# Five edits at the seams between the phases of one encoder step

## The chip, the cores and the metric

One core of one Trainium2 chip runs the whole step as one program. Its five engines take their instructions in order, each from its own list: TensorE (PE in the profile, with its weight loads as PEld), VectorE (DVE), ScalarE (ACT), GpSimd (POOL) and SyncE (SP), which here does nothing but issue DMAs. The metric is device time in microseconds (us), the median of several runs.

## The reference, cut to what matters

One layer of a streaming encoder for 1024 prompt tokens and 8 samples of 16 tokens (1152 tokens, 9 blocks of 128, or 3 blocks t of 384):

```python
xn = rms_norm(x, norm_g)
u, g_pool, c_q, c_kv, k_r, g_mla = jnp.split(xn @ w_in, SPLIT_IDX, axis=-1)
pool_out = multiscale_pool(pool_hist, u, pos0, w_pool, pool_scale) * jax.nn.silu(g_pool)
q = (rms_norm(c_q, q_norm_g) @ w_uq).reshape(B, T, N_HEADS, D_NOPE + D_ROPE)
q_nope = rms_norm(q[..., :D_NOPE], q_nope_g)
q_rope = apply_rope(rms_norm(q[..., D_NOPE:], q_rope_g), cos[:, None], sin[:, None])
ckv_new = rms_norm(c_kv, kv_norm_g)
krope_new = apply_rope(rms_norm(k_r, k_rope_g), cos, sin)
ckv_all = jnp.concatenate([ckv_hist, ckv_new], axis=1)
kv = (ckv_all @ w_ukv).reshape(B, S, N_HEADS, D_NOPE + D_V)
k_nope = rms_norm(kv[..., :D_NOPE], k_nope_g)
attn = chunk_causal_attention(q_nope, q_rope, k_nope, krope_all, v, q_pos, jnp.arange(S))
mla_out = attn.reshape(B, T, D_MLA) * jax.nn.silu(g_mla)
h = x + jnp.concatenate([pool_out, mla_out], axis=-1) @ w_out
gate = jax.nn.sigmoid(rms_norm(h, ple_norm_g) @ w_ple_gate + b_ple_gate)
y = h + gate * (p @ w_ple)
```

`multiscale_pool` takes, for 4 groups of 256 channels, the mean over the last 2, 4, 8 or 16 tokens minus the token, and a 256x256 matrix for each group (the mixer). For the samples, 1024 past tokens come from a cache. All values are float32.

## The kernel before

**Precision.** Each fp32 operand is split into two halves in TensorE's reduced fp32 format: ScalarE casts the high half (L68, or L71 with a gain) and VectorE subtracts it from the source for the low half (L69, L72). Each product is then three matmuls (`mm3`, L77 to L79; in the input projection L175 to L177). [...]

**Input projection (`phase1`).** Weights stand as 128x128 blocks, tokens stream in blocks of 384. The 16 blocks of the inner dimension are taken in two chunks of 8, `chunk(0, ...)` and then `chunk(1, ...)`. In a chunk, two column tiles of the weight and two token blocks make a 2x2 block product, done with seven products instead of eight (`Quick.pair`), on sums and differences of the operands; the third token block is multiplied plainly by `X` (8 tiles, `last_block`). Chunk 0's results go to DRAM (`part1`) and come back as `q` in chunk 1 (`prior`), where ScalarE adds them into PSUM ahead of the product (L192). The operands of chunk 1 (seven kinds `OPS`, four tiles each) are made during chunk 0, stored to DRAM as `sums`, and loaded between the chunks through four tiles `a0` to `a3`, each kind's tile j through `aj` (L506); `put` splits them. `X` of chunk 1 follows, loaded through the three tiles `o`, which also hold the evictions.

**The end of a product (`finish`).** VectorE adds the part of chunk 0, or multiplies by the norm factor `R2` for the third token block (L531); `gp` and `gm` get a SiLU on ScalarE (L537) and are stored from ScalarE's queue, `u`, `cq` and `ckv` from GpSimd's (L539).

**Mixer (`Pool`).** In chunk 1, `mixer(m, i)` is called at up to four places i of each pair m. From m = 5 on, each second pair adds the steps of one mixer group g to a list, at i = 0, and each call takes two steps from it. The steps load `u` from DRAM (L708 and on), compute the windows on VectorE (`d`), split `d` into `dh` and `dl`, load the gates `gp` into `ev` (L720), multiply on TensorE into `aux` (12 matmuls for each token block), and store `mixp` from GpSimd's queue. The last products of the third token block are held back (`held`) so that they stand behind the mixer and run to the end of the phase.

**Keys and queries (`phase2`).** For each block j of 128 tokens: `keys(j)` makes keys and values in banks `pb` (5 banks) and stores `vv`; `keys_out` transposes keys over `pt` (2 banks) and stores `kT`; `queries(j)`, `queries_out`, `rotary_out` do the like for queries and store `qT` and `qrT`. All these stores go out on SP's queue. The weights `w_uq` come in eight loads through two tiles `raw` and are split into `wqh`, `wql`. The embedding product `p @ w_ple` (`Embed.block`, banks `p`, evictions L803, loads on ScalarE's queue) is put between the blocks as filler.

**Attention.** `attend_samples` starts with the cache of the samples: `cache_T` is loaded on SP, cast to `ch` and `cl`, and multiplied into `k`. At its end four groups g of two heads are multiplied by the value weights: the outputs of g = 0, 1 lie in bank 0 of `ob` and those of g = 2, 3 in bank 1; VectorE multiplies each by its gate (L1455). `attend_prompt` and `phase5` (output projection, gate) follow.

**What sets the order.** The program is traced as written, and a scheduler then simulates it and gives each engine one list, by when it thinks that each instruction can start. `tc.issue_after(ins)` says that what is traced in its block, on the engine of `ins`, is issued behind `ins`. DMAs are issued in the order of the list of the engine whose queue they are on, and a DMA whose data is not there yet holds up all behind it on that engine.

Of the kernel before, what the change touches and what calls it, by code (L numbers as in the profile page):

```python
# [1 line left out]

# [4 lines left out]
F32R = mybir.dt.float32r  # L7
# [12 lines left out]
P = 128  # L20
# [232 lines left out]
def phase1(k, sc):  # L253
# [35 lines left out]
    def o_tile():  # L289
        return k.t(xp, [P, TB], "o", bufs=3)  # L290
# [10 lines left out]
    def last_block(c, j):  # L301

        i = 8 * c + j
        raw = (o_tile() if c else k.t(rp, [P, 2 * TB], f"x{j}"))[:, :TB]
        nc.sync.dma_start(raw, io["xT"][2][:, i, :])
        hl = [k.t(xp, [P, TB], f"X{j}{x}", F32R) for x in "hl"]
        k.split(hl[0][:], hl[1][:], raw, k.norm_g[:, i:i + 1])
        if c == 0:
            squares(R2, raw, raw)
        return hl  # L310
# [189 lines left out]
    chunk(0, None, keep, prepare)  # L500


    qk.tail()
    for n in OPS:
        for j in range(4):
            raw = k.t(ap, [P, TB], f"a{j}")  # L506
            nc.sync.dma_start(raw[:], sc["sums"][:, 4 * OPS.index(n) + j, :])
            put(n, j, raw[:])
    hs.close()
    X = [last_block(1, j) for j in range(8)]  # L510

    def prior(i, t):
        q = k.t(ep, [P, TB], "q", bufs=3)
# [10 lines left out]
    def finish(i, t, ps, q):  # L524
        kind, n = kinds[i] if i < KR else ("kr", 0)
        o = o_tile()
        if q is not None:
            nc.vector.tensor_tensor(o[:], ps, q[:], ALU.add)
            ps = o[:]
        if t == 2:  # L530
            nc.vector.tensor_tensor(o[:], ps, R2[:], ALU.mult)  # L531
        if kind == "kr":
            k.later(rope_key(k, lp, aux_bank, o, kc, ks, t, sc))
            return
        store = nc.gpsimd
        if kind in ("gp", "gm"):
            nc.scalar.activation(o[:], o[:], AF.Silu)  # L537
            store = nc.scalar
        store.dma_start(sc[kind][t][:, n, :], o[:])  # L539
        if kind not in ("ckv", "cq"):  # L540
            return
        if (kind, t) not in acc:
            acc[kind, t] = [k.t(lp, [P, TB], f"acc{t}"), 2 if kind == "ckv" else 4]
            nc.scalar.activation(acc[kind, t][0][:], o[:], AF.Square)
        else:
            sq = k.t(lp, [P, TB], "sq")
            nc.scalar.activation(sq[:], o[:], AF.Square)
            nc.vector.tensor_tensor(acc[kind, t][0][:], acc[kind, t][0][:], sq[:], ALU.add)
        acc[kind, t][1] -= 1
        if not acc[kind, t][1]:  # L550
            k.later(latent_factor(kind, t, acc[kind, t][0]))
# [1 line left out]
    lp = ls.enter_context(tc.tile_pool(name="p1c", bufs=1, side="right", reuse_waits="tile"))  # L553
    kc = k.t(lp, [P, 9, DR], "kc")
    ks = k.t(lp, [P, 9, DR], "ks")
    rope_tables(k, lp, kc, ks, io["k_rope_g2"], 1.0)
    mix = []


    def mixer(m, i):  # L560
        k.tick()
        if m < 5:
            return
        if not mix:
            assert not k.queue
            ls.close()
            mp = es.enter_context(tc.tile_pool(name="p1p", bufs=1, side="right", reuse_waits="tile"))
            inv = k.t(mp, [P, 16], "inv")
            nc.sync.dma_start(inv[:], io["inv_cnt"])
            mix.append(Pool(k, mp, aux_bank, inv, sc, wp))  # L570
            mix[0].zero = k.t(mp, [P, 16], "zero")
            nc.vector.memset(mix[0].zero[:], 0.0)
        pool = mix[0]
        if m in (5, 7, 9, 11) and i == 0:
            g = (m - 5) // 2
            for t in range(NT):
                if t == 0:
                    pool.fetch(2 * g, 0)
                steps.append(lambda t=t: (pool.fetch(2 * g + 1, t), t and pool.gates(g, t - 1), pool.tile(2 * g, t)))
                steps.append(lambda t=t: pool.tile(2 * g + 1, t))  # L580
                if t:
                    steps.append(lambda t=t: pool.mix(g, t - 1))
                else:
                    steps.append(lambda: pool.weights(g))
                steps.append(lambda t=t: (t < NT - 1 and pool.fetch(2 * g, t + 1), pool.split()))
                if t == NT - 1:
                    steps.append(lambda: (pool.gates(g, NT - 1), pool.mix(g, NT - 1)))
        step(2)
# [240 lines left out]
def phase2(k, sc, sh, fill):  # L829
# [70 lines left out]
    def keys(j):  # L900

        ch, cl, _ = ckv[j]
        kn = k.t(pw, [P, H, DN], "kn")
        vv = k.t(pw, [P, H, DN], "vv")
        for c in range(4):
            ps = bank("pb")
            w = (wk, wv)[c // 2]
            sl = slice((c % 2) * 512, (c % 2 + 1) * 512)
            for rt in range(2):
                k.mm3(ps[:], ch[:, rt, :], cl[:, rt, :], w[0][:, rt, sl], w[1][:, rt, sl], rt == 0, rt == 1)  # L910
            hs = slice(4 * (c % 2), 4 * (c % 2) + 4)
            src = ps[:].rearrange("p (h d) -> p h d", h=4)
            if c < 2:
                nc.scalar.activation(kn[:, hs, :], src, AF.Copy)
            else:
                nc.scalar.activation(vv[:, hs, :], src, AF.Copy)
        nc.sync.dma_start(sc["v"][:, :, j, :].rearrange("h p d -> p h d"), vv[:])
        r, = inv_norms(kn[:])
        halves(kn[:], r)
        return j, kn  # L920

    def keys_out(j, kn):
        kT = k.t(pw, [P, H, P], "T", bufs=2)
        for c in range(2):
            a = bank("pt")
            for i in range(4):
                nc.tensor.transpose(a[:, i * P:(i + 1) * P], kn[:, 4 * c + i, :], k.ident[:])
            nc.scalar.activation(kT[:, 4 * c:4 * c + 4, :], a[:].rearrange("p (h d) -> p h d", h=4), AF.Copy)
        nc.sync.dma_start(sc["kT"][:, :, j * P:(j + 1) * P].rearrange("h p q -> p h q"), kT[:])

    def queries(j):

# [16 lines left out]
    def queries_out(j, qn):  # L949
# [6 lines left out]
                nc.tensor.transpose(a[:, i * P:(i + 1) * P], qn[:, 4 * c + i, :DN], k.ident[:])  # L956
            nc.scalar.activation(qT[:, 4 * c:4 * c + 4, :], a[:].rearrange("p (h d) -> p h d", h=4), AF.Copy, scale=gqk[:])
        if j < 8:
            nc.sync.dma_start(sc["qT"][:, :, pos].rearrange("h p q -> p h q"), qT[:])
        return qT  # L960

    def rotary_out(j, qr):
# [79 lines left out]
    pp = es.enter_context(tc.tile_pool(name="p2p", bufs=1, space=PSUM, reuse_waits="tile"))  # L1042
    pq = es.enter_context(tc.tile_pool(name="p2c", bufs=1, reuse_waits="tile"))
    pw = es.enter_context(tc.tile_pool(name="p2b", bufs=1, reuse_waits="tile"))
    cq = {8: latent("cq", 8, 4, k.q_norm_g)}
    wq = [(k.t(pq, [P, 4, TB], f"wqh{g}", F32R), k.t(pq, [P, 4, TB], f"wql{g}", F32R)) for g in range(4)]
    for g in range(4):
        for i in range(2):
            sl = slice(2 * i, 2 * i + 2)
            k.split(wq[g][0][:, sl, :], wq[g][1][:, sl, :], raw_w([P, 2, TB], io["w_uq"][g][:, sl, :])[:])  # L1050
    ckv[8] = latent("ckv", 8, 2, k.kv_norm_g, "8", 1)
    qc = k.t(pq, [P, 9, DR], "qc")
    qs = k.t(pq, [P, 9, DR], "qs")
    rope_tables(k, pq, qc, qs, io["q_rope_g2"], SCALE)

    def key_steps(j):
        kp = keys(j)
# [231 lines left out]
def attend_samples(k, sc, sh, between, fill):  # L1289
# [149 lines left out]
    for g in range(4):  # L1439
# [2 lines left out]
        wvh = k.t(bp, [P, 2, 2 * DN], "wvh", F32R, bufs=3)  # L1442
        wvl = k.t(bp, [P, 2, 2 * DN], "wvl", F32R, bufs=3)
        k.split(wvh[:], wvl[:], raw[:])
        ps = ob[:, g // 2, g % 2 * 2 * P:(g % 2 + 1) * 2 * P].rearrange("p (a q) -> p a q", a=2)
        for i in range(2):
            h = 2 * g + i
            hs = slice(i * DN, (i + 1) * DN)
# [242 lines left out]
```

## Time and profile before

| | us |
|---|---|
| median of 3 runs | 2284.39 |
| lowest, highest | 2278.85, 2286.37 |
| profiled execution | 2275.97 |
| its span, first to last instruction | 2274.2 |

| engine | busy us | share of span |
|---|---|---|
| TensorE matmuls | 2199.2 | 97% |
| VectorE | 1438.0 | 63% |
| ScalarE | 1000.9 | 44% |
| GpSimd | 395.8 | 17% |

The mean granted TensorE clock is 0.992 of full speed. In a row of the waits, the name behind the arrow is the instruction that released the wait, by the profile. In a row of a timeline the first number is the start, the second the length, both in us; an x4 stands for four instructions in a run, and what stands in brackets is the idle time ahead of the row and what ended it. In a row of the table of stretches PEclk is the mean granted clock.

### The profile page before, as it was taken

Reading aid. Unit: us, or ns where it says so; the run is one execution under the profiler, and the core shown is the slowest. Engines: PE = TensorE matmul, PEld = TensorE weight load, DVE = VectorE, ACT = ScalarE, POOL = GpSimd, SP = SyncE. Lnnn points to the kernel's source line nnn. Section 1 sums busy time; section 2 is a strip of 40 time slices with the busy share of each in tenths; the row PEclk is TensorE's granted clock in tenths of the full one; section 3 lists DMA queues with packets and bytes.
Section 4 is the critical chain, followed back from the end, with each engine's and each line's share of the span. In section 5 each row is a group of like instructions: output and inputs, shape, how many; then the busy total and the mean of one; then the engine's idle time right before and its main releaser. Section 6 shows DMA issues by size and latency. Waiting matters only on the chain.

```text
span 2274.2 us, 35969 instructions
## 1 busy us (share of the span) xinstructions
PE 2199.2 (97%) x12856; PEld 2142.2 (94%) x12856; DVE 1438.0 (63%) x2993; ACT 1000.9 (44%) x2229; POOL 395.8 (17%) x391
## 2 busy tenths in 40 slices
PE   8999999999998999989999899999999999999999
PEld 7999999999998989979998799999999999999998
DVE  6767877786677668758888865555543345443343
ACT  6533335443333477766666743333342233232231
POOL 0000000101111001044543632211012221111110
PEclk9999999999999999999999999999999999999999
DMA  8535656457776666473222754443263333232221
GB/s 300 186 123 166 203 176 221 154 170 194 192 184 180 216 190 189 131 241 105 80 84 68 244 178 147 149 136 121 90 202 104 110 120 108 83 97 91 86 88 64
DMA packets 246005, 339.31 MB, mean 149 GB/s; under 512 B 38881, under 2 KB 192609, under 8 KB 245825
## 3 DMA queue, kind: packets, MB, share of 16 engines
q1 hardware_dynamic: 218720, 290.83, 41.6%
q10 hardware_dynamic: 19296, 23.21, 3.2%
q0 software_dynamic: 7808, 22.97, 3.1%
q8 instruction: 101, 1.65, 0.3%
q14 instruction: 80, 0.65, 0.1%
HBM read 235.74 MB, written 101.12 MB: 148 GB/s over the span
## 4 chain that ended last, share of the span: by engine, by line
PE 70%; DMA 12%; DVE 9%; issue 4%; ACT 3%; POOL 1%; SPq 1%; ACTq 0%; DVEq 0%; POOLq 0%
PE mm L77 8%; PE mm L79 8%; PE mm L78 8%; PE mm L175 6%; PE mm L176 6%; PE mm L177 6%; PE f L77 3%; PE f L79 3%; PE f L78 3%; PE k L78 2%; PE k L77 2%; PE k L79 2%; DMA u<-u 1%; PE t L1222 1%; DVE wl L69 1%
## 5 line engine op out<-in xcount | busy, mean ns | idle before, releaser
L68 ACT ACTIVATE wh<-wraw 128x1024 fp32r<-128x1024 f32 (+3 forms) x207 | 150.6, 729 | 138.4 <-PE mm L177 59.7
L69 DVE TENSOR_TENSOR wl<-wraw,wh 128x512 fp32r<-128x512 f32 (+3 forms) x205 | 172.8, 844 | 58.1 <-ACT wh L68 55.0
L1547 DVE TENSOR_TENSOR ev<-mm,R 128x384 f32<-128x384 f32 x48 | 26.7, 557 | 173.8 <-PE mm L79 169.9
L1548 ACT ACTIVATE ev<-ev,gains 128x384 f32<-128x384 f32 x48 | 29.4, 612 | 224.5 <-DVE ev L1547 124.4
L71 ACT ACTIVATE wh<-wraw,gains 128x128 fp32r<-128x128 f32 x256 | 82.1, 391 | 52.8 <-ACT wh L71 33.5
L77 PE MATMUL k<-wkh,ch 128*128 128x448 f32 x256 | 95.8, 375 | 4.7 <-ACT ch L68 4.1
L72 DVE SCALAR_TENSOR_TENSOR wl<-wraw,gains,wh 128x128 fp32r<-128x128 f32 x256 | 87.9, 389 | 18.0 <-ACT wh L71 17.0
L68 ACT ACTIVATE wh<-wt 128x1024 fp32r<-128x1024 f32 x60 | 63.5, 1058 | 80.8 <-PE mm L177 47.7
L69 DVE TENSOR_TENSOR wl<-wt,wh 128x1024 fp32r<-128x1024 f32 x60 | 73.4, 1224 | 38.1 <-ACT wh L68 38.0
L78 PE MATMUL k<-wkh,cl 128*128 128x448 f32 x256 | 94.0, 367 | 0.2 <-DVE cl L69 0.2
L79 PE MATMUL k<-wkl,ch 128*128 128x448 f32 x256 | 94.2, 368 | 0.0
L1223 ACT ACTIVATE pth<-t 128x512 fp32r<-128x512 f32 (+2 forms) x96 | 44.8, 485 | 102.6 <-PE t L1222 102.1
L79 PE MATMUL mm<-A2l,wh 128*128 128x384 f32 x256 | 86.0, 336 | 0.0
L78 PE MATMUL mm<-A2h,wl 128*128 128x384 f32 x256 | 86.0, 336 | 0.0
L77 PE MATMUL mm<-A2h,wh 128*128 128x384 f32 x256 | 86.0, 336 | 0.0
L77 PE MATMUL mm<-A0h,wh 128*128 128x384 f32 x256 | 85.8, 335 | 0.0
L79 PE MATMUL mm<-A0l,wh 128*128 128x384 f32 x256 | 85.7, 335 | 0.0
L78 PE MATMUL mm<-A1h,wl 128*128 128x384 f32 x256 | 85.7, 335 | 0.0
L78 PE MATMUL mm<-A0h,wl 128*128 128x384 f32 x256 | 85.7, 335 | 0.0
L77 PE MATMUL mm<-A1h,wh 128*128 128x384 f32 x256 | 85.5, 334 | 0.0
L79 PE MATMUL mm<-A1l,wh 128*128 128x384 f32 x256 | 85.5, 334 | 0.0
L1519 POOL TENSOR_TENSOR R<-R,sq 128x384 f32<-128x384 f32 x45 | 46.0, 1023 | 210.2 <-ACT sq L1518 205.2
(807 smaller groups left out, 7819.9 us busy)
## 6 DMA issues: line engine op xcount, KB each, us to landing
wraw<-w_in SPq DMA_DIRECT2D x89, 512.0 KB, 4.5
part<-o SPq DMA_DIRECT2D x93, 192.0 KB, 3.2
q<-part SPq DMA_DIRECT2D x93, 192.0 KB, 3.0
wraw<-w_out SPq DMA_DIRECT2D x64, 256.0 KB, 3.2
wraw<-w_ple_gate SPq DMA_DIRECT2D x64, 256.0 KB, 3.1
ple<-ev POOLq DMA_DIRECT2D x48, 192.0 KB, 2.9
fev<-xT SPq DMA_DIRECT2D x48, 192.0 KB, 2.5
hp<-fev SPq DMA_DIRECT2D x48, 192.0 KB, 2.3
```

Of the source, the lines that this page charges most:

```text
L68: nc.scalar.activation(hi, src, AF.Copy)
L69: eng.tensor_tensor(lo, src, hi, ALU.subtract)
L71: nc.scalar.activation(hi, src, AF.Copy, scale=scale)
L72: eng.scalar_tensor_tensor(lo, src, scale, hi, ALU.mult, ALU.subtract)
L77: mm(out, sh, mh, start=start, stop=False)
L78: mm(out, sl, mh, start=False, stop=False)
L79: self.last = mm(out, sh, ml, start=False, stop=stop)
L175: mm(ps, sh, xh[:], start=start and j == 0, stop=False, **kw)
L176: mm(ps, sl, xh[:], start=False, stop=False, **kw)
L177: self.k.last = mm(ps, sh, xl[:], start=False, stop=j == n - 1, **kw)
L1223: nc.scalar.activation(pth[:, :n, qq], tp[:, :n, :], AF.Copy)
L1519: nc.gpsimd.tensor_tensor(acc[t][:], acc[t][:], sq[:], ALU.add)
```

## The change

There are five edits.

1. Between the chunks, the 28 loads of `sums` and the 8 loads of `X` go through five tiles `a0`, `a1`, `a2`, `a3`, `as` in turn (`relay`), where the loads of `sums` had four tiles by their j, and `X` had the three tiles `o`. The tables for the keys' rotation are loaded and scaled in the mixer's first call of pair 1 instead of ahead of chunk 1.
2. A mixer group's steps enter the list at i = 2 of their pair instead of i = 0.
3. The queries' preparation (latent of block 8, the splits of `w_uq`, the tables of the queries' rotation) is issued on VectorE behind the last eviction of the input projection.
4. The stores of `v`, `kT` and `qT` go out on ScalarE's queue instead of SP's.
5. The outputs of the samples' group g go to bank g % 3.

```diff
--- before.py
+++ after.py
@@ -1,3 +1,4 @@
+import itertools
 from contextlib import ExitStack
 
 import concourse.bass as bass
@@ -301,7 +302,7 @@
     def last_block(c, j):
 
         i = 8 * c + j
-        raw = (o_tile() if c else k.t(rp, [P, 2 * TB], f"x{j}"))[:, :TB]
+        raw = (relay() if c else k.t(rp, [P, 2 * TB], f"x{j}"))[:, :TB]
         nc.sync.dma_start(raw, io["xT"][2][:, i, :])
         hl = [k.t(xp, [P, TB], f"X{j}{x}", F32R) for x in "hl"]
         k.split(hl[0][:], hl[1][:], raw, k.norm_g[:, i:i + 1])
@@ -500,14 +501,19 @@
     chunk(0, None, keep, prepare)
 
 
+    turn = itertools.cycle(["a0", "a1", "a2", "a3", "as"])
+
+    def relay():
+        return k.t(ap, [P, TB], next(turn))
+
     qk.tail()
     for n in OPS:
         for j in range(4):
-            raw = k.t(ap, [P, TB], f"a{j}")
+            raw = relay()
             nc.sync.dma_start(raw[:], sc["sums"][:, 4 * OPS.index(n) + j, :])
             put(n, j, raw[:])
+    X = [last_block(1, j) for j in range(8)]
     hs.close()
-    X = [last_block(1, j) for j in range(8)]
 
     def prior(i, t):
         q = k.t(ep, [P, TB], "q", bufs=3)
@@ -528,7 +534,7 @@
             nc.vector.tensor_tensor(o[:], ps, q[:], ALU.add)
             ps = o[:]
         if t == 2:
-            nc.vector.tensor_tensor(o[:], ps, R2[:], ALU.mult)
+            k.evicted = nc.vector.tensor_tensor(o[:], ps, R2[:], ALU.mult)
         if kind == "kr":
             k.later(rope_key(k, lp, aux_bank, o, kc, ks, t, sc))
             return
@@ -553,11 +559,12 @@
     lp = ls.enter_context(tc.tile_pool(name="p1c", bufs=1, side="right", reuse_waits="tile"))
     kc = k.t(lp, [P, 9, DR], "kc")
     ks = k.t(lp, [P, 9, DR], "ks")
-    rope_tables(k, lp, kc, ks, io["k_rope_g2"], 1.0)
     mix = []
 
 
     def mixer(m, i):
+        if (m, i) == (1, 0):
+            rope_tables(k, lp, kc, ks, io["k_rope_g2"], 1.0)
         k.tick()
         if m < 5:
             return
@@ -571,7 +578,7 @@
             mix[0].zero = k.t(mp, [P, 16], "zero")
             nc.vector.memset(mix[0].zero[:], 0.0)
         pool = mix[0]
-        if m in (5, 7, 9, 11) and i == 0:
+        if m in (5, 7, 9, 11) and i == 2:
             g = (m - 5) // 2
             for t in range(NT):
                 if t == 0:
@@ -914,7 +921,7 @@
                 nc.scalar.activation(kn[:, hs, :], src, AF.Copy)
             else:
                 nc.scalar.activation(vv[:, hs, :], src, AF.Copy)
-        nc.sync.dma_start(sc["v"][:, :, j, :].rearrange("h p d -> p h d"), vv[:])
+        nc.scalar.dma_start(sc["v"][:, :, j, :].rearrange("h p d -> p h d"), vv[:])
         r, = inv_norms(kn[:])
         halves(kn[:], r)
         return j, kn
@@ -926,7 +933,7 @@
             for i in range(4):
                 nc.tensor.transpose(a[:, i * P:(i + 1) * P], kn[:, 4 * c + i, :], k.ident[:])
             nc.scalar.activation(kT[:, 4 * c:4 * c + 4, :], a[:].rearrange("p (h d) -> p h d", h=4), AF.Copy)
-        nc.sync.dma_start(sc["kT"][:, :, j * P:(j + 1) * P].rearrange("h p q -> p h q"), kT[:])
+        nc.scalar.dma_start(sc["kT"][:, :, j * P:(j + 1) * P].rearrange("h p q -> p h q"), kT[:])
 
     def queries(j):
 
@@ -956,7 +963,7 @@
                 nc.tensor.transpose(a[:, i * P:(i + 1) * P], qn[:, 4 * c + i, :DN], k.ident[:])
             nc.scalar.activation(qT[:, 4 * c:4 * c + 4, :], a[:].rearrange("p (h d) -> p h d", h=4), AF.Copy, scale=gqk[:])
         if j < 8:
-            nc.sync.dma_start(sc["qT"][:, :, pos].rearrange("h p q -> p h q"), qT[:])
+            nc.scalar.dma_start(sc["qT"][:, :, pos].rearrange("h p q -> p h q"), qT[:])
         return qT
 
     def rotary_out(j, qr):
@@ -1042,16 +1049,18 @@
     pp = es.enter_context(tc.tile_pool(name="p2p", bufs=1, space=PSUM, reuse_waits="tile"))
     pq = es.enter_context(tc.tile_pool(name="p2c", bufs=1, reuse_waits="tile"))
     pw = es.enter_context(tc.tile_pool(name="p2b", bufs=1, reuse_waits="tile"))
-    cq = {8: latent("cq", 8, 4, k.q_norm_g)}
-    wq = [(k.t(pq, [P, 4, TB], f"wqh{g}", F32R), k.t(pq, [P, 4, TB], f"wql{g}", F32R)) for g in range(4)]
-    for g in range(4):
-        for i in range(2):
-            sl = slice(2 * i, 2 * i + 2)
-            k.split(wq[g][0][:, sl, :], wq[g][1][:, sl, :], raw_w([P, 2, TB], io["w_uq"][g][:, sl, :])[:])
-    ckv[8] = latent("ckv", 8, 2, k.kv_norm_g, "8", 1)
-    qc = k.t(pq, [P, 9, DR], "qc")
-    qs = k.t(pq, [P, 9, DR], "qs")
-    rope_tables(k, pq, qc, qs, io["q_rope_g2"], SCALE)
+
+    with tc.issue_after(k.evicted.ins):
+        cq = {8: latent("cq", 8, 4, k.q_norm_g)}
+        wq = [(k.t(pq, [P, 4, TB], f"wqh{g}", F32R), k.t(pq, [P, 4, TB], f"wql{g}", F32R)) for g in range(4)]
+        for g in range(4):
+            for i in range(2):
+                sl = slice(2 * i, 2 * i + 2)
+                k.split(wq[g][0][:, sl, :], wq[g][1][:, sl, :], raw_w([P, 2, TB], io["w_uq"][g][:, sl, :])[:])
+        ckv[8] = latent("ckv", 8, 2, k.kv_norm_g, "8", 1)
+        qc = k.t(pq, [P, 9, DR], "qc")
+        qs = k.t(pq, [P, 9, DR], "qs")
+        rope_tables(k, pq, qc, qs, io["q_rope_g2"], SCALE)
 
     def key_steps(j):
         kp = keys(j)
@@ -1442,7 +1451,7 @@
         wvh = k.t(bp, [P, 2, 2 * DN], "wvh", F32R, bufs=3)
         wvl = k.t(bp, [P, 2, 2 * DN], "wvl", F32R, bufs=3)
         k.split(wvh[:], wvl[:], raw[:])
-        ps = ob[:, g // 2, g % 2 * 2 * P:(g % 2 + 1) * 2 * P].rearrange("p (a q) -> p a q", a=2)
+        ps = ob[:, g % 3, :2 * P].rearrange("p (a q) -> p a q", a=2)
         for i in range(2):
             h = 2 * g + i
             hs = slice(i * DN, (i + 1) * DN)
```

On TensorE, in the input projection's chunk 1, the mixer's group 0 stands like this before: its third token block's 12 matmuls (into `aux`) begin in the middle of a product by `X` (into `mm`), 31 instructions behind the first of its second token block.

```order
L175 MATMUL mm_5755<-X2h_3873,wh_5336 128x384
L77 MATMUL aux_5837<-dh_1151_5804,pwh_5488 128x384
L78 MATMUL aux_5837<-dh_1151_5804,pwl_5489 128x384
L176 MATMUL mm_5755<-X2h_3873,wl_5337 128x384
L177 MATMUL mm_5755<-X2l_3874,wh_5336 128x384
L175 MATMUL mm_5755<-X3h_3879,wh_5336 128x384
L176 MATMUL mm_5755<-X3h_3879,wl_5337 128x384
L177 MATMUL mm_5755<-X3l_3880,wh_5336 128x384
L175 MATMUL mm_5755<-X4h_3885,wh_5336 128x384
L176 MATMUL mm_5755<-X4h_3885,wl_5337 128x384
L79 MATMUL aux_5837<-dl_1152_5805,pwh_5488 128x384
```

With the change they begin behind a whole product, 84 instructions behind the first of the second block's.

```order
L176 MATMUL mm_5630<-S_3h_3853,wh_5353 128x384
L177 MATMUL mm_5630<-S_3h_3853,wl_5354 128x384
L178 MATMUL mm_5630<-S_3l_3854,wh_5353 128x384
L78 MATMUL aux_5988<-dh_1156_5852,pwh_5538 128x384
L79 MATMUL aux_5988<-dh_1156_5852,pwl_5539 128x384
L80 MATMUL aux_5988<-dl_1157_5853,pwh_5538 128x384
L78 MATMUL aux_5988<-dh_1158_5856,pwh_5538 128x384
L79 MATMUL aux_5988<-dh_1158_5856,pwl_5539 128x384
```

The 12 matmuls of a token block now stand together, with 36 matmuls of the projection between the first two blocks and 72 between the second and the third. The groups 1, 2 and 3 move alike.

On VectorE, at the end of the input projection, the last two evictions (L531) stand like this before, with the queries' tables (`qc`, `qs`), a split of `w_uq` (`wql`) and a latent (`rawcq`) between them and ahead of them:

```order
L69 TENSOR_TENSOR wvl_7977<-raw_8001,wvh_7976 128x2x512
L622 SCALAR_TENSOR_TENSOR qc_8322<-qc_8322,ropeg_8324 128x576
L622 SCALAR_TENSOR_TENSOR qs_8323<-qs_8323,ropeg_8324 128x576
L531 TENSOR_TENSOR o_8192<-mm_8164,R_48_127 128x384
L69 TENSOR_TENSOR wql_1645_8272<-raw_8279,wqh_1644_8271 128x768
L853 SCALAR_TENSOR_TENSOR rawcq_8571<-rawcq_8571,gains_132,srow_8572 128x128 x4
L531 TENSOR_TENSOR o_8224<-mm_8196,R_48_127 128x384
L69 TENSOR_TENSOR wql_1645_8272<-raw_8283,wqh_1644_8271 128x768
```

With the change (line numbers are some 6 higher) the two evictions stand ahead of all these:

```order
L70 TENSOR_TENSOR wvl_7977<-raw_8001,wvh_7976 128x2x512
L537 TENSOR_TENSOR o_8192<-mm_8164,R_48_127 128x384
L537 TENSOR_TENSOR o_8224<-mm_8196,R_48_127 128x384
L860 SCALAR_TENSOR_TENSOR rawcq_8259<-rawcq_8259,gains_132,srow_8260 128x128 x4
L70 TENSOR_TENSOR wql_1645_8272<-raw_8279,wqh_1644_8271 128x768
L70 TENSOR_TENSOR wql_1645_8272<-raw_8283,wqh_1644_8271 128x768
L860 SCALAR_TENSOR_TENSOR rawckv_1660_8311<-rawckv_1660_8311,gains_132,srow_8312 128x128 x2
L629 SCALAR_TENSOR_TENSOR qc_8322<-qc_8322,ropeg_8324 128x576
```

What is ahead of the evictions now is the second split of the values' weights, `wvl`.

On SP, at the end of the keys and queries, the last stores and the first load of the samples' cache stand like this before:

```order
L959 DMA qT_103<-T_10425 128x8x128
L929 DMA kT_101<-T_10439 128x8x128
L971 DMA qrT_104<-rT_10684 128x4x128
L959 DMA qT_103<-T_10692 128x8x128
L1321 DMA raw_10727<-cache_T 128x2x512
L1327 DMA kraw_10733<-cache_krT 64x512 x2
```

With the change:

```order
L978 DMA qrT_104<-rT_10684 128x4x128
L1330 DMA raw_10727<-cache_T 128x2x512
L1336 DMA kraw_10733<-cache_krT 64x512 x2
L978 DMA qrT_104<-rT_10706 128x4x128
L1330 DMA raw_10888<-cache_T 128x2x512
```

The load of `cache_T` now stands directly behind the store of `qrT`; the stores of `kT` and `qT` stand on ScalarE's list, among the casts and evictions that write their data. SP's list has 1175 rows instead of 1200, ScalarE's 1816 instead of 1791.

## The prediction

> **What bounds the kernel now.** I read the engines' busy shares first, then the waits of TensorE, the granted clock in the stretches around the largest waits, and last the timelines of the engine that is late at each.
>
> ```profile
> span 2274.2 us, 35969 instructions
> PE 2199.2 (97%) x12856; PEld 2142.2 (94%) x12856; DVE 1438.0 (63%) x2993; ACT 1000.9 (44%) x2229; POOL 395.8 (17%) x391
> ```
>
> TensorE is busy for 2199.2 of 2274.2 us. No edit changes a matmul, so all that can be won lies in the other 75 us and in stretches in which the clock is low. The waits, in us, times, longest:
>
> ```profile
> PE aux L77 <- ACT dh L68: 13.5, 6, 4.3
> PE pb L77 <- ACT wqh L68: 6.8, 1, 6.8
> ...
> PE k L77 <- ACT ch L68: 4.1, 1, 4.1
> ...
> PE p L77 <- ACT ev L803: 3.7, 7, 0.8
> PE k L77 <- DVE gate L1455: 3.6, 2, 2.1
> ...
> PE mm L175 <- ACT s L206: 2.3, 1, 2.3
> ...
> PE mm L175 <- ACT X4h L71: 1.6, 1, 1.6
> ```
>
> These rows sum to 35.6 us, and each belongs to one edit: the mixer (13.5), the last eviction (6.8), the samples' cache and the filler before it (4.1 + 3.7), the outputs' banks (3.6), the seam between the chunks (2.3 + 1.6). Behind the longer of them the clock is low too:
>
> ```profile
> 387.00:391.00 4.00, 4.00 (x16) 4.00 (x16) 2.16 (x5) 1.79 (x5) 0.00 (x0) 0.60 0.94 312
> ...
> 614.00:620.00 6.00, 5.98 (x21) 5.99 (x22) 3.94 (x7) 0.38 (x1) 0.54 (x1) 0.59 0.82 263
> ...
> 741.00:746.00 5.00, 5.00 (x21) 4.68 (x20) 4.97 (x13) 2.00 (x3) 0.00 (x0) 0.66 0.49 155
> ...
> 780.00:793.00 13.00, 13.00 (x77) 13.00 (x76) 7.47 (x18) 5.12 (x8) 0.00 (x0) 1.00 0.85 259
> ...
> 801.00:806.00 5.00, 5.00 (x13) 3.84 (x13) 2.70 (x6) 2.77 (x6) 0.00 (x0) 0.50 0.90 298
> ...
> 991.00:996.00 5.00, 4.82 (x18) 3.88 (x19) 2.58 (x4) 3.60 (x11) 2.16 (x2) 0.66 0.84 252
> ```
>
> The columns are the stretch, its length, the busy time of PE, PEld, DVE, ACT and POOL (with the instructions), and PEclk, followed by the DMA share and GB/s. At 780 the clock is full and 77 matmuls take 13.00 us, 0.169 each. In the others TensorE is as good as busy, but at PEclk 0.60, 0.59, 0.66, 0.50 and 0.66. Length times what the clock lacks gives 4.0 x 0.40 = 1.6, 6.0 x 0.41 = 2.5, 5.0 x 0.34 = 1.7, 5.0 x 0.50 = 2.5 and 1.7 us: 10.0 us of lost work. They go with the waits. [...]
>
> **The mixer, half a pair later.** The largest of its waits, on SP and then ACT:
>
> ```profile
> 605.58 0.33 SPq L720 DMA_DIRECT2D ev<-gp  x1
> 606.00 0.38 SPq L514 DMA_DIRECT2D q<-part  x1
> ```
>
> ```profile
> 612.06 0.49 ACT L192 ACTIVATE mm<-q 128x384 f32<-128x384 f32 x1 [6.01 <-DMA q<-part]
> ...
> 613.46 0.92 ACT L68 ACTIVATE dh<-d 128x384 fp32r<-128x384 f32 x2
> ```
>
> A gate's load `ev` needs a buffer that the mixer's last store gives back; the load of `q` stands behind it on SP, ScalarE waits 6.01 us for `q`, and the casts `dh` stand behind that on ScalarE. TensorE then meets the mixer's matmuls in the middle of the projection's. So two lists in order hold each other up. The edit adds no work: it puts the same loads, casts and stores half a pair later; in the new order the casts stand ahead of the L192 that waits, more loads of `q` stand ahead of the gate's load, and 72 matmuls of the projection stand between the second and third block instead of 19. At 0.169 us each these 53 more give 9.0 us of lead, against a wait of 4.3 at most. Upper bound: all of 13.5 us and 2.5 + 1.7 of clock, 17.7. Lower bound: only the two waits of about 4 with their clock are mended in half, some 6. The order is clean, so I am near the top: **14 us**. What is late next is `q` itself, which now shares SP with the gates at another place; that keeps me from 17.7.
>
> **The queries' work behind the last eviction.** VectorE before TensorE's wait of 6.8 us:
>
> ```profile
> 792.98 1.23 DVE L69 TENSOR_TENSOR wvl<-raw,wvh 128x1024 fp32r<-128x1024 f32 x1 [1.96 <-ACT wvh L68]
> ...
> 797.53 0.96 DVE L69 TENSOR_TENSOR wql<-raw,wqh 128x768 fp32r<-128x768 f32 x1 [1.52 <-ACT wqh L68]
> 798.91 1.14 DVE L853 SCALAR_TENSOR_TENSOR rawcq<-rawcq,gains,srow 128x128 f32<-128x128 f32 x4 [0.43 <-DMA rawcq<-cq]
> 799.97 0.55 DVE L531 TENSOR_TENSOR o<-mm,R 128x384 f32<-128x384 f32 x1
> ```
>
> The wait is put down to the cast `wqh`, but what TensorE needs is the bank that the last L531 gives back at 800.52. It stands behind `wql` and `rawcq`, which wait for DMAs. With them behind it, only the second `wvl` is ahead (ends 794.21); two evictions of 0.55 end at 795.31. TensorE starts 5.2 us earlier, its wait shrinks to 1.6, and the 2.5 us of clock stay full: 7.7 us at first.
>
> It does not keep all. The eight splits `wql` wait for eight loads through two tiles:
>
> ```profile
> L69 DVE TENSOR_TENSOR wql<-raw,wqh x8: 948/956/959, 797.5 to 824.1; 128x768 fp32r<-128x768 f32 x8
> L79 PE MATMUL pb<-wql,cqh x33: 334/334/343, 815.9 to 835.0; 128*128 128x384 f32 x33
> ```
>
> ```profile
> 801.65 0.33 SPq L841 DMA_DIRECT2D raw<-w_uq  x1
> ...
> 818.18 0.53 SPq L841 DMA_DIRECT2D raw<-w_uq  x1
> ```
>
> The splits begin at 797.5 and the last at 824.1, 3.8 us for each, and the first products that read them run from 815.9 on: a TensorE that comes 7.7 us earlier reaches the last splits before their loads, for the loads are paced by two tiles and not by VectorE's list. Bounds: nothing left, or all 7.7. Filler stands between the query's products and hides a part; I take about half, **4 us**.
>
> **Stores on ScalarE's queue.** SP, ScalarE and TensorE at the end of the phase:
>
> ```profile
> 974.43 0.36 SPq L971 DMA_DIRECT2D qrT<-rT  x1
> 981.13 0.36 SPq L959 DMA_DIRECT2D qT<-T  x1
> 981.58 0.73 SPq L1321 DMA_DIRECT2D raw<-cache_T  x1
> ```
>
> ```profile
> 989.77 1.06 ACT L68 ACTIVATE ch<-raw 128x1024 fp32r<-128x1024 f32 x1 [4.08 <-DMA raw<-cache_T]
> ```
>
> ```profile
> 990.88 1.08 PE L77 MATMUL k<-wkh,ch 128*128 128x448 f32 x2 [4.13 <-ACT ch L68]
> ```
>
> The load of `cache_T` waits on SP behind a store `qT`, whose transposes are late; it goes out at 981.58 and its data is there at 989.77, 8.2 us later. With the store gone the load goes out behind `qrT`, at about 974.8, and the data is there at 983.0. The cast ends at 984.1, before 986.75, where TensorE's wait begins (990.88 less 4.13). In the new order, though, 30 matmuls of the filler stand between those transposes and the first product of the cache, where 42 stood: 12 x 0.169 = 2.0 us less cover, of the 2.7 us that lie between 984.1 and 986.75. The filler's own waits (3.7 us, 7 times, for the eviction of its banks) lie in the same stretch; what is won there is cover lost too, so I book nothing for them, and of the 4.1 us and 1.7 of clock 5.0: **5 us**; upper bound 4.1 + 1.7 + 3.7 = 9.5.
>
> Against that stand 25 DMAs more on ScalarE's list, at 0.36 us each 9.0 us of its time, in this stretch:
>
> ```profile
> 800.00:987.00 187.00, 182.08 (x1024) 167.78 (x1024) 139.66 (x444) 138.19 (x475) 14.97 (x32) 0.98 0.57 172
> ```
>
> ScalarE is busy 138.19 of 187.00 us there, and TensorE idle only 4.9. ScalarE's slack of 48.8 hides the 9.0 as long as the five `pb` banks let TensorE run ahead; with that cover gone it costs all 9.0 and the wait is won or not: the bounds of this edit are -9 and 9.5. [...]
>
> **Between the chunks.** ScalarE and TensorE:
>
> ```profile
> 385.54 0.52 ACT L68 ACTIVATE S_2h<-a 128x384 fp32r<-128x384 f32 x1 [0.27 <-DMA a<-sums]
> 385.96 0.47 ACT L206 ACTIVATE s<-mm 128x384 f32<-128x384 f32 x1
> ```
>
> ```profile
> L507 SPq DMA_DIRECT2D a<-sums x24: 319/376/438, 352.0 to 385.2; - x24
> ```
>
> The eviction `s` stands behind a cast that waits for `a`. The loads follow each other in (385.2 - 352.0) / 23 = 1.4 us, paced by four tiles; a fifth lets each go up to 1.4 us earlier. So 1.4 of the 2.3 go; the 1.6 for `X4h`, whose tile is one of three `o` that evictions hold too, go whole; and of 1.6 us of clock 1.0: **4 us**, between 0 (SP's stores of `part` stand among the loads) and 5.5. The rotation's tables, moved to the first pair's call, are a few instructions on VectorE (63% busy): nothing.
>
> **The outputs' banks.** 3.6 us are put down to the gate. Its neighbours:
>
> ```profile
> 1269.61 1.50 DVE L69 TENSOR_TENSOR pl<-pv,ph 128x256 fp32r<-128x256 f32 x1
> 1271.04 0.41 DVE L1455 TENSOR_TENSOR gate<-k,gate 128x256 f32<-128x256 f32 x1
> ```
>
> ```profile
> 1271.60 0.30 PE L77 MATMUL k<-ph,wvh 128*128 128x128 f32 x1 [1.52 <-DVE gate L1455]
> ```
>
> The product's own operand `pl` ends at 1271.11, so without the gate TensorE would start 0.4 us earlier at most: **1 us** for both places, bounds 0 and 3.6.
>
> **Sum.** 14 + 4 + 5 + 4 + 1 = 28 us off the profiled execution's 2275.97: 2248. The median of the runs shown is 8.4 us above the profiled one, so the forecast for a median is 2284.39 - 28 = **2256 us**.
>
> **Rivals.** *Everything named goes:* 17.7 + 7.7 + 9.5 + 5.5 + 3.6 = 44.0, 2240 us. For it: no edit adds work, and TensorE is 97% busy. Against: the w_uq loads, and `pl`. *The waits change place:* the loads now stand at the end of each chain: `q` behind the gates again (half of the mixer, 7), nothing at the queries (w_uq's two tiles), 2 at the cache, 1 at the chunks, 0 at the banks: 10 us, 2274. For it: 8.2 us for a load of `cache_T` and 6.01 for `q`, transfers that no edit shortens. Against: the mixer's new lead of 53 matmuls. *The change doesn't do what it says:* the scheduler's list moves the mixer's waits to the next pair at the same size and only the last eviction and the cache gain, some 5 us: 2279, no change. *Slower, by ScalarE's queue:* 24 of the stores stand ahead of evictions on ScalarE. Each holds up what is behind it by its 0.36 us and by the end of the cast that writes its data (1.06 us for a cast above), 1.4 in all; if `pb` and `pt` run dry each time, 24 x 1.4 = 34 us, more than the 28: 2290. It decides from 28 / 24 = 1.2 us for each store. Against it: ScalarE's slack of 48.8 us and TensorE's idle time of 4.9, which says that five banks were enough so far.
>
> **How the numbers follow.** Chances: the forecast 0.50 (its own range 2246 to 2266), everything 0.10, the waits change place 0.18, not what it says 0.12, slower 0.10. The range leaves out the slower half of the last and most of what lies beyond everything: 2240 to 2281. A measurement of this kernel can tell about 0.3%, 7 us, from no change: faster is below 2277.5, slower above 2291.2. Faster 0.50 + 0.10 + 0.16 = 0.76, same 0.16 (with the slower case's near half and what it takes from the change of place), slower 0.08.
>
> **What would show it.** In the changed profile TensorE's wait for `dh` should be below 4 us in all; the last two evictions should follow `wvl` within 1.5 us, and a new wait of 2 to 5 us should stand at `wql` some 25 us later; `cache_T` should go out right behind `qrT`, with a wait of 2 to 3 us before the first product of the cache; the waits at `s` and `X4h` should be below 1 us together, and those at the gate should become waits for `pl`. The clock should be full at all five places. I am wrong if TensorE's waits between 800 and 980 grow (ScalarE's queue), or if the mixer's 13.5 us come back under another name.

## The result

| | kernel before | changed |
|---|---|---|
| median of 4 runs, us | 2283.1 | 2263.74 |
| lowest, highest | 2278.85, 2286.37 | 2260.6, 2266.43 |
| profiled execution | 2275.97 | 2263.17 |

The ratio is 0.9919, with a 95% interval of 0.9902 to 0.9936: 0.8% faster, some 18 us. The forecast was 28 us less, a median of 2256; the range, 2240 to 2281, holds the result.

TensorE is as busy as before, in a span that is 12.8 us shorter. From the page of the changed kernel (line numbers are 1 to 9 higher than before):

```profile
span 2261.4 us, 35981 instructions
...
PE 2197.8 (97%) x12856; PEld 2139.6 (95%) x12856; DVE 1433.5 (63%) x2993; ACT 1001.4 (44%) x2229; POOL 394.9 (17%) x391
```

TensorE's waits in the changed kernel, those that answer to the ones of before and the new ones:

```profile
PE mm L176 <- DVE o L534: 4.2, 1, 4.2
PE k L78 <- DVE gate L1464: 3.6, 2, 2.1
...
PE p L78 <- ACT ev L810: 2.9, 6, 0.9
...
PE aux L78 <- ACT dh L69: 2.0, 2, 1.0
...
PE mm L176 <- ACT s L207: 1.7, 2, 1.3
...
PE mm L176 <- ACT X7h L72: 1.4, 1, 1.4
...
PE pb L78 <- DVE o L537: 0.7, 1, 0.7
...
PE k L78 <- ACT ch L69: 0.5, 1, 0.5
```

The waits for `dh` fell from 13.5 to 2.0 us, the one at the last eviction from 6.8 to 0.7, the one for `ch` from 4.1 to 0.5. The one for the gate is what it was, 3.6. And a wait of 4.2 us is new: `o`, at the first matmul of a product.

Both executions issue the same 12856 matmuls, so the time at which the n-th starts can be compared. At a few places where both are in the same product, the changed kernel's start less the other's:

| place | n | difference, us | won in the stretch | forecast |
|---|---|---|---|---|
| chunk 0, no edit in it | 1900 | +3.55 | -3.55 | 0 |
| behind the seam of the chunks | 2500 | +0.84 | 2.7 | 4 |
| end of the projection | 4250 | -3.78 | 4.6 | 14 |
| first products of the keys | 4300 | -10.11 | 6.3 | 4 for this and the next |
| end of keys and queries | 5300 | -7.33 | -2.8 | |
| in the samples' products | 5400 | -12.25 | 4.9 | 5 |
| end | 12855 | -12.77 | 0.5 | 1 |

Chunk 0 runs the same code in both, and its 3.55 us are of the execution: from 18 to 25 us the granted clock is 0.51 in the changed kernel's profile and 1.00 in the other. Without them the profiles show 16.3 us, where the forecast had 28. Most of the gap is one term: the mixer, 4.6 instead of 14.

That 4.6 is of one pair of executions. A second profile of the changed kernel, `e_again` below, on another chip, is 0.66 us ahead of the profile of before at the end of chunk 0 and 18.47 at the end of the projection, 14.3 of it in the mixer's stretch. No kernel before was profiled on that chip, whose median before is 13 us lower, so chip and edit can't be told apart there.

**Where the mixer's gain went.** In the pair of profiles, on ScalarE, behind the mixer's last casts, and on TensorE:

```profile
729.57 0.49 ACT L193 ACTIVATE mm<-q 128x384 f32<-128x384 f32 x1 [6.98 <-DMA q<-part]
```

```profile
732.02 0.69 PE L176 MATMUL mm<-S_0h,wh 128*128 128x384 f32 x1 [4.16 <-DVE o L534]
```

It is the same wait as before, `q` for ScalarE, 6.98 us where it had been 6.01, at the last group instead of the second, and TensorE now meets it at a bank that VectorE has not yet evicted (`o`) instead of at `dh`. Two loads of `q` had gone out in time, SP's row says, and the transfers of that stretch, with their time to landing, say why they came late:

```profile
719.06 1.77 SPq L520 DMA_DIRECT2D q<-part  x2
```

```profile
q<-part SPq DMA_DIRECT2D x2, 192.0 KB, 9.3
gm<-o ACTq DMA_DIRECT2D x1, 192.0 KB, 9.7
npool<-us POOLq DMA_DIRECT2D x1, 60.0 KB, 10.6
npool<-u POOLq DMA_DIRECT2D x1, 7.5 KB, 9.6
```

`q` takes 9.3 us, against a median of 3.4 over the execution. `npool<-us` is the store of the samples' new pooling state: 60 KB, written from a tile in which 15 values (60 bytes) lie together, so 1024 pieces. The table by stretch, as in the prediction:

```profile
717.00:722.00 5.00, 5.00 (x31) 5.00 (x30) 4.97 (x9) 3.03 (x6) 1.45 (x2) 1.00 1.07 146
722.00:728.00 6.00, 5.26 (x29) 4.61 (x27) 3.71 (x8) 0.59 (x1) 1.10 (x2) 1.00 1.04 110
...
732.00:738.00 6.00, 5.98 (x19) 5.98 (x20) 5.93 (x16) 2.40 (x4) 0.00 (x0) 0.50 0.52 158
776.00:790.00 14.00, 14.00 (x82) 13.75 (x80) 6.50 (x11) 5.06 (x7) 0.00 (x0) 1.00 0.90 280
```

From 717 to 728 all DMA engines are occupied (share 1.07 and 1.04) and move 146 and 110 GB/s; from 776 to 790 a smaller share of 0.90 moves 280. Behind the wait the clock is 0.50 for 6 us: 3.0 us of lost work. Earlier, from 665 to 670 us, it is 0.66: 1.7 more. So from 540 to 790 us TensorE's waits went from 15.7 to 9.9 us, and the lost work from 4.2 (2.5 and 1.7 before) to 4.7, which comes near the 4.6 us won. That the small pieces are the cause was my estimate, and left to the runs.

### The profile page after: what moved, and what is told of

Same layout as the page of the kernel before. It is cut to its first block, busy times and chain, and to the rows that moved or that the text cites. A ratio compares the mean times of both kernels' runs of the same rounds, so it can differ in the third digit from the quotient of the medians.

```text
span 2261.4 us, 35981 instructions
## 1 busy us (share of the span) xinstructions
PE 2197.8 (97%) x12856; PEld 2139.6 (95%) x12856; DVE 1433.5 (63%) x2993; ACT 1001.4 (44%) x2229; POOL 394.9 (17%) x391
## 4 chain that ended last, share of the span: by engine, by line
PE 72%; DMA 10%; DVE 9%; issue 5%; ACT 2%; POOL 1%; SPq 0%; ACTq 0%; DVEq 0%; POOLq 0%
PE mm L78 8%; PE mm L80 8%; PE mm L79 8%; PE mm L176 7%; PE mm L177 7%; PE mm L178 7%; PE f L78 3%; PE f L80 3%; PE f L79 3%; PE k L78 2%; PE k L80 2%; PE k L79 2%; DMA u<-u 2%; PE t L1231 1%; DVE wl L70 1%
```

## The experiments

The runs were on several chips, whose kernel before had medians of 2283.1, 2272.39, 2270.34 and 2280.72 us, so only ratios to the kernel before on the same chip are compared. The first four:

**The mixer's edit alone.** The kernel before with

```diff
-        if m in (5, 7, 9, 11) and i == 0:
+        if m in (5, 7, 9, 11) and i == 2:
```

> The kernel before with the mixer's edit alone. Theory of the prediction, mis-sized (the edit removes the waits for dh but leaves a new wait of about 4 us plus 3 us of low clock at the last group): 4 to 6 us below the kernel before, about 2278. Rival, that the edit alone is worth the 14 us I booked and the other edits take some back: about 2269. In the profile the first theory wants TensorE's waits for dh below 4 us in all and one new wait of about 4 us behind a late load of q; the second wants no wait over 2 us between 540 and 790.

Measured: ratio 0.9994, 0.9984 to 1.0005: nothing, 2270.89 against 2272.39 us. The two largest rows of TensorE's waits between 540 and 790 us, and then the largest between 800 and 900:

```profile
PE mm L175 <- DVE o L528: 3.6, 1, 3.6
PE aux L77 <- ACT dh L68: 1.2, 1, 1.2
```

```profile
PE pb L77 <- ACT qn L939: 2.9, 1, 2.9
```

The waits for `dh` are down to 1.2 and the new one is there, as the first theory wanted. Counted by matmuls, this execution gains 9.7 us on the profile of before (of another chip) across the mixer, and loses 4.4 of it again in the queries, where a new wait of 2.9 stands, and 4.6 behind the samples. So the edit alone is worth less than either theory said.

**All but the mixer's edit** (the same line back to `i == 0` in the changed kernel).

> The changed kernel with the mixer's steps back at i = 0. If the edits simply add, with the 4.6 us that the two profiles show for the mixer's stretch, this is 4 to 6 us above the changed kernel: about 2269. If the mixer's edit is worth 14 us, about 2278; if it is worth nothing, 2264. The waits for dh should come back at 13 to 14 us in the profile.

Measured: ratio 0.9962, 0.9947 to 0.9977, so 0.4 to 0.5% slower than the changed kernel: some 11 us, between the two sizes that I had put. The waits for `dh` stand at 9.5 us in its profile, not quite the 13 to 14 expected.

**Without the stores of the state.** The changed kernel, with the samples' new pooling state left unwritten, less

```diff
-            nc.gpsimd.dma_start(io["npool"][ct][:, 1:, :], us[:, :, NS:])
```

> The changed kernel without the eight stores of the samples' new pooling state (60 KB each in runs of 60 bytes); that output is left unwritten. Theory 'small packets': these stores keep all DMA engines busy for some 6 us each while little is moved, and the loads of q behind them land after 9 us instead of 3. Then the wait of 4.2 us and its low clock (3 us) go, and some of the smaller waits: 6 to 10 us below the changed kernel, about 2256. Rival 'order of the lists': the load of q is late because of what stands ahead of it on SP; nothing changes, within 2 us of 2264, and q still lands after 9 us.

Measured: ratio 0.9889, 0.9872 to 0.9907. Against the changed kernel's 0.9919 that is 0.3%, 7 us, as 'small packets' wanted, though the two intervals just touch (0.9902 to 0.9936 for the changed kernel). All of TensorE's waits from 540 to 790 us that the trace lists:

```profile
PE p L78 <- ACT wh L69: 1.1, 1, 1.1
PE pb L78 <- DVE o L537: 0.7, 1, 0.7
PE pb L78 <- ACT kn L920: 0.7, 1, 0.7
PE mm L176 <- DVE u L222: 0.3, 1, 0.3
```

None of the mixer's is left; three of the four belong to the keys behind it. In the traces the lists of TensorE, VectorE and SP are row for row those of the changed kernel, and ScalarE's is up to 830 us, behind the mixer; GpSimd's has the eight stores less. So the order on SP was not what made `q` late.

**The state in long runs.** The changed kernel with

```diff
-            us = self.us[ct] = k.t(self.pp, [P, NB, HIST + NS], "us", bufs=2)
-            nc.sync.dma_start(us[:, :, :HIST], self.k.io["state_pool"][ct])
+            st = self.us[ct] = k.t(self.pp, [P, 9, HIST], "st", bufs=2)
+            nc.sync.dma_start(st[:, 1:, :], self.k.io["state_pool"][ct])
...
-            nc.gpsimd.dma_start(io["npool"][ct][:, 0, :], u[:, n:n + HIST])
-            us = self.us.pop(ct)
+            st = self.us.pop(ct)
+            us = k.t(pp, [P, NB, HIST + NS], "us")
+            nc.gpsimd.tensor_copy(us[:, :, :HIST], st[:, 1:, :])
...
-            nc.gpsimd.dma_start(io["npool"][ct][:, 1:, :], us[:, :, NS:])
+            np = k.t(pp, [P, 9, HIST], "st", bufs=2)
+            nc.gpsimd.tensor_copy(np[:, 0, :], u[:, n:n + HIST])
+            nc.gpsimd.tensor_copy(np[:, 1:, :], us[:, :, NS:])
+            nc.gpsimd.dma_start(io["npool"][ct], np[:])
```

> The changed kernel with the samples' pooling state loaded and stored through a tile in which a channel's values lie together (runs of 480 and 540 bytes instead of 60), with three small copies on GpSimd for each of the eight column tiles. 'Small packets': loads and stores land within 4 us instead of 7 to 10, and the time is 6 to 12 us below the changed kernel, about 2255. 'Order of the lists': within 3 us of 2264, or above it if the copies on GpSimd make its stores later.

Measured: ratio 0.9888, 0.9864 to 0.9911, with every output written. It is the time without the stores (0.9889) again, so the loads of the state add nothing that can be told. The landing of `st` and of the one store that is left, least, median and longest, and TensorE by stretch:

```profile
DMA to landing us min/median/max: 1.8/2.9/4.4
```

```profile
540.00:690.00 150.00, 150.00 (x860) 150.00 (x860) 119.91 (x228) 55.00 (x88) 30.90 (x57) 1.00 0.68 209
690.00:720.00 30.00, 30.00 (x173) 30.00 (x172) 28.63 (x59) 13.75 (x24) 4.04 (x9) 1.00 0.67 204
```

TensorE does not stop once from 540 to 720 us, at full clock. The transfers that took 7 us at the median and up to 10.6 take 2.9 and 4.4.

The next four ran on one chip, the changed kernel itself among them.

> The changed kernel itself, to stand beside the next three on one chip. By the two profiles 0.8% below the kernel before: ratio 0.990 to 0.994.

Measured: ratio 0.9912, 0.9899 to 0.9925: the result, once more. The new wait is there too, 2.6 us in this execution; in the four other profiles with the steps at i = 2 and the short pieces, on two chips, it is 2.9 to 3.9.

**Without the tiles in turn** (the loads of `sums` through `a0` to `a3` by j, `X` through `o`, the tables ahead of chunk 1):

```diff
-            raw = relay()
+            raw = k.t(ap, [P, TB], f"a{j}")
...
-        raw = (relay() if c else
+        raw = (o_tile() if c else
```

> The changed kernel with the tiles a0 to a3 by their j and X through o again. The profiles show 2.7 us for that stretch: 2 to 4 us above the changed kernel. Rival: the seam is paced by the loads whatever the tiles, within 1 us; then the wait for s before 12_0h is as long as without the edit's undoing.

Measured: ratio 0.9930, 0.9918 to 0.9942, 0.2% or some 4 us slower than the changed kernel, as expected. Waits at the seam, 375 to 405 us, first without the edit:

```profile
PE mm L175 <- ACT X4h L71: 2.2, 1, 2.2
PE mm L175 <- ACT s L206: 1.7, 1, 1.7
PE mm L175 <- ACT X2h L71: 1.2, 1, 1.2
```

and with it, on the same chip:

```profile
PE mm L176 <- ACT X7h L72: 0.9, 1, 0.9
PE mm L176 <- ACT mm L193: 0.6, 1, 0.6
PE mm L176 <- ACT X2h L72: 0.2, 1, 0.2
```

5.1 us of waits against 1.7.

**Without the queries' work behind the eviction:**

```diff
-    with tc.issue_after(k.evicted.ins):
-        cq = {8: latent("cq", 8, 4, k.q_norm_g)}
+    cq = {8: latent("cq", 8, 4, k.q_norm_g)}
```

> The changed kernel with the queries' preparation no longer behind the last eviction. The profiles show 6.3 us won at the seam, of which 2.8 are lost again within the next 180 us: 3 to 5 us above the changed kernel, with the wait of 7 us back. Rival: all of it is lost again because the weights' loads set the pace, then within 1 us.

Measured: ratio 0.9951, 0.9939 to 0.9963: 0.4%, about 9 us, twice what I expected. The wait is back:

```profile
PE pb L78 <- ACT wqh L69: 6.1, 1, 6.1
```

**Without ScalarE's queue** (the three stores back to `nc.sync`).

> The changed kernel with the stores of v, kT and qT on SP again. The profiles show 4.9 us won at the samples' cache: 4 to 6 us above the changed kernel, and the wait for ch of 4 us back. Rival, that ScalarE's list pays for the stores: equal or below the changed kernel.

Measured: ratio 0.9975, 0.9963 to 0.9987: 0.6%, some 14 us, three times the term. Not one place shows it. The wait for `ch` is not back at 4 us:

```profile
PE p L78 <- ACT ev L810: 4.0, 7, 1.2
PE pb L80 <- DVE sql L70: 2.3, 1, 2.3
PE pt L975 <- ACT T L935: 1.2, 1, 1.2
PE k L78 <- ACT ch L69: 0.9, 1, 0.9
```

By matmuls this execution loses, against the changed kernel's on the same chip, 5 us in the queries, 2 at the cache, 6 from the samples' end to the start of the prompt's attention, 3 in the mixer and 4 before any edit begins. Undoing the four edits one by one costs about 4, 9, 14 and 11 us, 38 in all, of a change that is worth 18 to 20: they are not terms of a sum.

**The last four** ask what is left of the five edits once the transfers are short. *The kernel before with the state in long runs, and none of the edits* (the diff of the state in long runs):

> The kernel before with the samples' pooling state loaded and stored in long runs, and none of the five edits. If the mixer's waits before the change were the slow transfers and not the place of its steps, the waits for dh (13.5 us) and their low clock go without moving anything: 12 to 18 us below the kernel before, ratio about 0.993. If their place was the cause, the waits stay and the ratio is 0.998 or more.

Measured: ratio 0.9932, 0.9917 to 0.9947, 15 us off. The two largest rows of TensorE's waits from 540 to 790 us:

```profile
PE pb L77 <- ACT wqh L68: 5.8, 1, 5.8
PE aux L77 <- ACT dh L68: 1.3, 2, 0.8
```

13.5 us for `dh` became 1.3 with the steps where they were.

*The changed kernel with long runs and the mixer's steps at i = 0:*

> The changed kernel with the state in long runs and the mixer's steps back at i = 0. If place matters once the transfers are short, this is 5 us or more above the run with both (ratio 0.9888 to the kernel before on its chip); if it does not, it is within 3 us of it.

Measured: ratio 0.9890, 0.9873 to 0.9906, against 0.9888 with the steps at i = 2. The place makes no difference then:

```profile
PE aux L78 <- ACT dh L69: 0.3, 1, 0.3
```

Against the run before it, on the same chip (0.9932), the four other edits together bring 0.4%, some 10 us: that is what is left of the change once the transfers are short.

*The changed kernel with long runs and the samples' outputs in two tiles:*

```diff
-        ps = ob[:, g % 3, :2 * P].rearrange("p (a q) -> p a q", a=2)
+        ps = (k.t(pp, [P, 512], "aux")[:, :2 * P] if g % 2 else ob[:, g // 2, :2 * P]).rearrange("p (a q) -> p a q", a=2)
```

> The changed kernel with the state in long runs, and the samples' outputs of the groups 1 and 3 in another tile of PSUM instead of another bank of the same tile. TensorE's wait at the first product of groups 1 and 3 is then for pl and not for the gate: 0.4 us shorter at each place. At most 1 us below the run without the other tile, not to be told apart in the time: ratio about 0.988. In the profile no wait for the gate is left. Rival, that the gate was the whole wait: the 3.6 us go.

Measured: ratio 0.9875, 0.9859 to 0.9891, not to be told from 0.9888, but with the long runs clear of the changed kernel's 0.9912 (0.9899 to 0.9925). The waits, with three banks of one tile in the run with long runs, and then with two tiles:

```profile
PE k L78 <- DVE gate L1467: 2.1, 2, 1.5
```

```profile
PE aux L80 <- DVE pl L70: 1.8, 2, 0.9
```

2.1 us for the gate became 1.8 us for `pl`, the operand.

*The stores alone on ScalarE's queue*, in the kernel before:

> The kernel before with the stores of v, kT and qT alone on ScalarE's queue. The undoing of this edit in the changed kernel cost 16.7 us, my term was 5. If the edit is worth its 5 us by itself, the ratio is about 0.998; if it is worth 15 or more by itself, 0.993 or less; if it is worth that much only beside the others, near 1.

Measured: ratio 0.9975, 0.9965 to 0.9984: 5.7 us, the 5 of the term. So most of the other 9 us that its undoing cost come only beside the other edits.

## Why the prediction was right, and where it was not

**What bounds the kernel.** Right: TensorE does the same work, and the time went only out of its waits and its low clock. At the seam, the last eviction and the cache the stretches of low clock are gone; in the mixer's part two others stand, behind the new wait of 4.16 us and from 665 to 670 us. At the seam of the chunks, where the longest wait is now 1.4 us, the clock is full:

```profile
384.00:391.00 7.00, 6.41 (x37) 5.86 (x35) 5.85 (x10) 4.76 (x10) 0.00 (x0) 1.00 0.92 263
```

From 665 to 670 us it is not: there it is 0.66, behind waits of 0.97, 0.70 and 0.21 us. The forecast's terms for the clock took it that a shorter wait leaves the clock full; no run shows that as a rule. In this profile it is 1.00 at the seam (384 to 402 us), the last eviction (786 to 806) and the cache (980 to 996), with waits of 1.4, 0.7 and 0.5 us, and in the mixer's part 0.50 behind 4.16 us and 0.66 behind 0.97 and less.

**The mixer, 14 us: 4.6 in the pair of profiles, and the step that failed is the lead.** "These 53 more give 9.0 us of lead, against a wait of 4.3 at most" took the casts' place for the cause and the wait for `q` as given. It took the order of the lists, "two lists in order hold each other up", as the mechanism. The cause was the transfer: `q` on its way for 9.3 us while stores in pieces of 60 bytes hold the DMA engines (share 1.07 and 1.04); without those stores `q` takes 7.3 us at the longest instead of 9.7, and the ratio is 0.9889. The edit moved the place at which TensorE meets it. Alone it is worth nothing (0.9994), though its undoing in the changed kernel costs some 11 us; with short transfers its place makes no difference (0.9890 and 0.9888); and the transfers alone give 15 us (0.9932), the 14 that I had put down to the move. Two rows of the trace of before could have told it, the time to landing (least, median, longest) of what concerns the tile `us`, the state, and of what concerns `q`:

```profile
DMA to landing us min/median/max: 3.4/7.1/12.2
```

```profile
DMA to landing us min/median/max: 2.3/3.0/12.6
```

A transfer of 60 KB that takes 7.1 us, beside one of 192 KB that takes 3.0 and at worst 12.6, is one to look into. The lead itself was read from one group: in the last, where the new wait stands, the third block's matmuls begin 76 instructions behind the second's before and 48 after, so that group does not move like the others.

**The last eviction, 4 us: right.** It follows `wvl` as forecast:

```profile
787.27 1.23 DVE L70 TENSOR_TENSOR wvl<-raw,wvh 128x1024 fp32r<-128x1024 f32 x1 [1.87 <-ACT wvh L69]
788.41 0.55 DVE L537 TENSOR_TENSOR o<-mm,R 128x384 f32<-128x384 f32 x1
790.11 0.56 DVE L537 TENSOR_TENSOR o<-mm,R 128x384 f32<-128x384 f32 x1 [1.15 <-PE mm L178]
```

The last one even waits for TensorE now. 6.3 us were won at the place and 2.8 lost again in the next 180 us, 3.5 in all. The give-back is there, but not at `wql`, where the prediction had put it:

```profile
L70 DVE TENSOR_TENSOR wql<-raw,wqh x8: 946/958/960, 791.6 to 819.2; 128x768 fp32r<-128x768 f32 x8
```

The last split starts 4.9 us earlier, where TensorE is 9.9 earlier, and no wait of 2 to 5 us stands there (0.3 for `wqh`). What is lost is spread over small waits, 1.2 for `sql` the largest; that the loads' pace is behind them is not shown. In the experiment the edit's undoing cost 9 us, more than the 3.5.

**ScalarE's queue, 5 us: right, 4.9 in the profiles and 5.7 alone.** The load is behind `qrT`, as the order said:

```profile
971.67 0.36 SPq L978 DMA_DIRECT2D qrT<-rT  x1
972.12 1.04 SPq L1330 DMA_DIRECT2D raw<-cache_T  x1
```

The wait left is 0.5 us, not 2 to 3. The rival that ScalarE pays for the stores fell: the edit's undoing makes the kernel slower. One sign against the edit did show, TensorE's waits between 800 and 985 us: without the one at the last eviction they grew from 3.3 to 7.3. With the stores back on SP they are 9.5, so ScalarE's queue is not their cause. The traces show 24 stores moved, not 25.

**Between the chunks, 4 us: right**, 2.7 in the pair of profiles and about 4 by the undoing; the longest of the waits that were to be below 1 us together is 1.4.

**The banks, 1 us: the edit does nothing to its wait,** and the forecast was off by its whole. TensorE's first product of a group still waits for the gate, 3.6 us in both profiles; with long runs it is 2.1 with the old banks and with the new. So the wait is kept for the tile and not for the bank; with two tiles it goes, and then `pl` holds TensorE almost as long, which was the prediction's reason for 1 us and not 3.6.

**The rivals.** The waits changed place in the mixer, the one edit whose lead I had put against that rival, and the result lies between the forecast and the rival's 2274. That it still lies in the forecast's own range (2246 to 2266) is in part luck: the largest term had the wrong cause, and the terms do not add up.

What stays open: why the edits undone one by one cost twice what they bring together. Each run's losses lie in several stretches, also some without an edit, and single executions differ there by 1 to 4 us. The profiled execution without the queries' work behind the eviction is the fastest of its five and loses 4.6 us against `e_again`, the one without ScalarE's queue the slowest of its twelve and loses 18.7. A part can be seen in the clock. Its mean over the profiled execution is 0.991 without the mixer's edit and 0.991 without ScalarE's queue, against 0.995 in both profiles of the changed kernel; 0.4% of spans of 2268.7 and 2268.4 us is some 9 us of lost work each, an estimate from these means that does not say in which stretches it lies. And the clock differs between executions of one kernel: 0.991 to 0.996 in the nine without the mixer's edit, 0.990 to 0.994 in the twelve without ScalarE's queue.

## What to carry to other kernels

A wait at the end of a chain of lists in order looks like a matter of order. Before moving work, look at how long the load at its start was on its way, against that load's median; where it is well above the median (here 9.3 us against 3.4), look for transfers in short pieces beside it (here of 60 bytes, at a DMA share of 1.07 and 146 GB/s), and lengthen the pieces. And after moving outputs to other banks, look in the waits whether the old one is still there: here it was kept for the tile, and another bank of the same tile did not free it (2.1 us with the old banks and with the new).

## What the runs showed of the hardware

Eight stores and eight loads of 60 KB, under 1 MB of the 339 that the kernel moves, went in the changed kernel with loads of 192 KB that took 9.3 us, against a median of 3.4, at a DMA share of 1.07 and 1.04 and 146 and 110 GB/s. Three GpSimd copies for each of the eight column tiles, of 0.2 to 0.5 us at the median, in place of the short pieces brought the state's loads and stores to 2.9 us at the median, and the kernel before 15 us (ratio 0.9932). TensorE's clock was low behind long waits and behind short ones: in the changed kernel 0.50 from 732 to 738 us behind one of 4.16 us and 0.66 from 665 to 670 behind 0.97 us and less, in the kernel before 0.60 from 387 to 391 behind one of 2.3. And the chips differ: the same kernel before had medians from 2270 to 2283 us, 0.6%, as much as most of the edits are worth.
